# Hybrid SSD and attention layer on one core: 64-row tiles padded to 128 rows, the y half of the out-projection ahead of the norm, one-bank PSUM tiles, and a new issue order up to the FFN

## Chip, core and metric

The kernel runs on one core of one Trainium2 chip. The metric is the device time of one execution in microseconds (us). The engines are named as in the profile: PE (TensorE, matrix products), PEld (its weight loads), DVE (VectorE), ACT (ScalarE), POOL (GpSimd) and SP (SyncE, which here only issues DMAs).

## The reference

One layer is computed for 512 frames of a new stream and 64 frames of a running one, 576 tokens in all, with a model width of 1024:

```python
h = rmsnorm(x, p['norm_mix']);  proj = h @ p['w_in']          # z, xbc, dt, cq, ckv
xbc, conv_new = causal_conv(xbc, conv_buf, ...)               # 4 taps, then silu
y, h_new = ssd_scan(xh, dt, A, Bm, Cm, ssm_h0)                # 8 heads of 64, state 128
y = (y + d_skip * xh) * silu(z);  y_ssd = rmsnorm(y, p['ssd_norm'])
q = rmsnorm(cq, q_norm) @ p['w_uq'];  q_rope, k_rope = apply_rope(...)
o = mla_attend(...) @ w_uv                                    # 8 heads, keys: 256 cached + new
x = x + concat([y_ssd, o]) @ p['w_out']
x = x + (silu(hf @ w_gate) * (hf @ w_up)) @ w_down            # hf = rmsnorm(x), width 2816
```

The outputs are the normed x, the compressed keys, the rotated keys, the SSD states and the last rows ahead of the convolution. Everything is fp32.

## The kernel before

The activations lie transposed: channels on the 128 partitions, the 576 tokens along the free dimension. A product of full precision is made of three f32r matmuls: the weight and the activation are each split in a high and a low part, and high x high, high x low and low x high are added in PSUM (`product`, L123, and `product_halves`, L450). `split_weights` (L107) casts the high part on ACT and subtracts it on DVE for the low part. The SSD and the attention use plain fp32 matmuls.

The work runs in stages, each a string of step names that `steps` (L273) goes through:

- **Start and inputs (0 to about 87 us).** The first products with the norm of x (`norm_factor`, L189, gives R1), the small product for dt and the rotary key, then eight input tiles (`in_tile`, L285) with the convolution (`conv_tile`, L388), the step sizes (`step_sizes`, L342), and the rotary part of the queries (`q_rope`, L425). PSUM tiles come from a pool psA with two buffers of two banks each (`mm_tile`, L157): one tile holds both token halves, side by side.
- **SSD (to about 148 us).** Four z tiles and five chunks of 128 tokens, of which chunk 4, the running stream, has 64 (`chunk_a` L482, `chunk_e`, `chunk_b`, `chunk_s`); between them the first query and key projections of the attention (`pair_proj`).
- **Attention (to about 221 us).** `norm_y` (L758) makes the norm factor Ry of y, `cat_tile` (L763) multiplies y by gain and factor and splits it into cat_y. For each pair p of heads come the scores `S`, whose softmax (`soft`, L648) takes the maximum on DVE and the exponential on ACT; the transposes of the probabilities (`turn` T, `turn_s` t); the values (`values` V, `values_s` W). `F` is the y half of the out-projection for one of eight output tiles (`out_tile((0,), t)`, L738). PSUM has three banks for scores ("sc"), three for transposes and values ("pp") and two for projections ("hm"), each released by the DVE or ACT instruction that reads it. values_s works on 64 query rows; its first key block has 64 rows, the others 128.
- **Out-projection (to about 250 us)** with the attention half, added on x2 (loaded from x by SP, `load_x2` L769), and the y half of tile 1; beside it the FFN's first weight splits.
- **FFN (to about 597 us)** and the last product and norm. Nothing in these is changed.

The order in which each engine issues its instructions is written out: the table `ISSUE` holds, for each engine, the places of its instructions in program order, and `issue_in_order` (L1305) chains them. So an engine's queue is fixed, and an instruction that waits holds up what stands behind it on that engine.

## Time and profile before

| | |
|---|---|
| time, median of 3 runs | 635.02 us (634.54 to 635.94) |
| span of the profiled execution | 633.0 us |
| its PE busy time, share of the span | 622.7 us, 98% |
| DVE | 539.3 us, 85% |
| ACT | 400.4 us, 63% |
| POOL | 117.7 us, 19% |

What lies between the span and the median of the runs is 2.0 us. A row of the timeline has the start, the duration, the engine, the line, the operation, the tile written and the tiles read, the tile of the array (rows*columns), the shape and the count; a bracket at the end is the engine's idle time before it and what ended it. An fp32 matmul has two records in the trace.

### The profile page before, as it was taken

The numbers are of one execution on the slowest core, as the hardware profiler recorded it, in microseconds if no ns is written. First come the engines' busy times: TensorE is split into PE (matmuls) and PEld (weight loads), VectorE is DVE, ScalarE is ACT, GpSimd is POOL, SyncE is SP. The second block draws the span as 40 slices with busy tenths as digits, with TensorE's granted clock in tenths as the row PEclk, the third lists the DMA queues.
The fourth block names the chain that finished last, engine by engine and source line by source line (L and its number), as shares of the span: only waits on it lengthen the run. The fifth ranks groups of instructions, "written<-read, shape, count | busy, mean of one in ns | idle before, by whom it ended". The sixth has DMA issues, their size and how long they took to land.

```text
span 633.0 us, 12094 instructions
## 1 busy us (share of the span) xinstructions
PE 622.7 (98%) x4635; PEld 596.3 (94%) x4635; DVE 539.3 (85%) x939; ACT 400.4 (63%) x768; POOL 117.7 (19%) x170
## 2 busy tenths in 40 slices
PE   9999999999999999999999999999999999999995
PEld 9899999986787899999999999999999999999995
DVE  6999986789776699999999888988899789976555
ACT  7655346779775567666556676566657665767364
POOL 1322104231010000001301330033104220323323
PEclk9999999999999999999999999999999999999999
DMA  8322374413231223335743986397738893689924
GB/s 320 134 61 74 95 193 127 128 61 106 77 117 34 96 72 126 89 106 178 262 128 90 221 182 152 82 193 185 169 100 162 199 202 101 100 215 251 256 41 149
DMA packets 39593, 89.19 MB, mean 141 GB/s; under 512 B 4570, under 2 KB 14312, under 8 KB 39280
## 3 DMA queue, kind: packets, MB, share of 16 engines
q1 hardware_dynamic: 26416, 63.12, 31.0%
q0 software_dynamic: 12400, 24.73, 21.3%
q8 instruction: 36, 0.59, 0.4%
q10 hardware_dynamic: 720, 0.57, 0.3%
q14 instruction: 21, 0.17, 0.1%
HBM read 62.74 MB, written 24.53 MB: 138 GB/s over the span
## 4 chain that ended last, share of the span: by engine, by line
PE 88%; DVE 6%; ACT 2%; issue 2%; POOL 1%; DMA 1%; POOLq 0%; DVEq 0%
PE ps_x L874 21%; PE ps_d L1064 14%; PE ps_z L874 10%; PE ps_in L281 7%; PE ps_y L874 5%; PE ps_o L458 4%; PE ps_z L458 4%; PE ps_first L129 3%; PE ps_d L281 2%; PE sc L672 2%; PE ps_p L874 2%; PE ps_l L281 2%; PE pv L719 1%; PE ptp L694 1%; PE ps_q L458 1%
## 5 line engine op out<-in xcount | busy, mean ns | idle before, releaser
L874 PE MATMUL ps_x<-xop,wh_gu_S 128*128 128x288 f32 x378 | 76.9, 295 | 0.0
L112 DVE TENSOR_TENSOR wl_gu_S<-gu,wh_gu_S 128x1024 fp32r<-128x1024 f32 x44 | 53.3, 1220 | 9.1 <-ACT wh_gu_S L111 6.2
L874 PEld LDWEIGHTS ps_x<-xop,wh_gu_S 128*128 128x128 f32 x378 | 60.5, 188 | 0.0
L1078 POOL DMA_DIRECT2D acc<-fz x32 | 27.9, 902 | 166.5 <-ACT fz L1075 137.8
L111 ACT CAST wh_gu_S<-gu 128x1024 fp32r<-128x1024 f32 x44 | 46.3, 1053 | 16.3 <-PE ps_y L874 8.3
L874 PE MATMUL ps_x<-xop,wl_gu_S 128*128 128x288 f32 x189 | 55.8, 295 | 0.0
L281 PE MATMUL ps_in<-xs,wh_in 128*128 128x256 f32 (+1 forms) x256 | 51.2, 296 | 0.4 <-DVE sp_a L361 0.4
L281 PEld LDWEIGHTS ps_in<-xs,wh_in 128*128 128x128 f32 x256 | 40.8, 188 | 1.2 <-issue 1.1
L281 PE MATMUL ps_in<-xs,wl_in 128*128 128x320 f32 (+1 forms) x128 | 37.7, 295 | 0.0
L874 PEld LDWEIGHTS ps_x<-xop,wl_gu_S 128*128 128x128 f32 x189 | 35.6, 188 | 0.0
L111 ACT CAST wh_gu_A<-gu 128x1024 fp32r<-128x1024 f32 x22 | 23.1, 1050 | 10.6 <-PE ps_x L874 7.2
L874 PE MATMUL ps_z<-xop,gu_a 128*128 128x288 f32 x189 | 29.5, 294 | 0.0
L458 PE MATMUL ps_o<-cat_y,wh_out 128*128 128x256 f32 (+1 forms) x128 | 28.9, 311 | 0.5 <-DVE cat_y L145 0.3
L112 DVE TENSOR_TENSOR wl_gu_A<-gu,wh_gu_A 128x1024 fp32r<-128x1024 f32 x22 | 26.8, 1218 | 1.5 <-ACT wh_gu_A L111 1.3
L1023 POOL DMA_DIRECT2D acc<-dn x8 | 4.4, 544 | 121.5 <-ACT dn L1022 121.5
L874 PE MATMUL ps_x<-xop_last,wh_gu_S 128*128 128x288 f32 x126 | 26.9, 295 | 0.0
L874 PEld LDWEIGHTS ps_z<-xop,gu_a 128*128 128x128 f32 x189 | 26.5, 188 | 0.0
L1064 PE MATMUL ps_d<-pair,d_1h 128*128 128x288 f32 x128 | 26.4, 296 | 0.0
L874 PE MATMUL ps_z<-xop,wh_gu_S 128*128 128x288 f32 x126 | 26.0, 295 | 0.0
L458 PE MATMUL ps_z<-xs,wh_z 128*128 128x256 f32 (+1 forms) x128 | 25.8, 296 | 0.1
L874 PE MATMUL ps_y<-xop,wh_gu_A 128*128 128x288 f32 x126 | 25.8, 296 | 0.0
L458 PE MATMUL ps_o<-cat_o,wh_out 128*128 128x320 f32 (+1 forms) x128 | 25.4, 294 | 0.3 <-DVE x L750 0.3
(418 smaller groups left out, 2164.1 us busy)
## 6 DMA issues: line engine op xcount, KB each, us to landing
gu<-in_w_gu SPq DMA_DIRECT2D x44, 512.0 KB, 5.3
wr_d<-in_w_down SPq DMA_DIRECT2D x18, 512.0 KB, 4.2
acc<-fz POOLq DMA_DIRECT2D x16, 288.0 KB, 7.2
acc<-da POOLq DMA_DIRECT2D x16, 288.0 KB, 8.0
acc<-dc POOLq DMA_DIRECT2D x16, 288.0 KB, 8.5
wr_in<-in_w_in SPq DMA_DIRECT2D x8, 512.0 KB, 3.8
wr_out<-in_w_out SPq DMA_DIRECT2D x8, 512.0 KB, 3.4
cumb<-cumD SPq DMA_DIRECT2D x5, 512.0 KB, 4.0
```

The costliest lines, as they stand in the source:

```text
L111: act.copy(hi, raw)
L112: dve.tensor_tensor(lo, raw, hi.bitcast(F32), ALU.subtract)
L129: pe.matmul(ps[:m, hf, : cols.stop - cols.start], w, x[:, cols], start=start and k == 0 and i == 0, stop=stop and k == last and i == 2,)
L281: pe.matmul(ps, w, x[:, cols], start=first and k == 0 and i == 0, stop=last and k == len(terms) - 1 and i == 2,)
L458: pe.matmul(ps[:, :n], w, x[:, cols], start=k == 0 and i == 0, stop=k == len(terms) - 1 and i == 2,)
L672: pe.matmul(s[:, :nk], qs[:, j, q0 : q0 + P], ks[:, j, :nk], start=True, stop=True)
L694: pe.transpose(pp[:, k : k + P], prs[p, i][:, j, b * P : b * P + P], ident)
L719: pe.matmul(pv[64 * j : 64 * j + 64, b * P :], V[b][:, h * HD : (h + 1) * HD], pts[p, b, j], start=b == 0, stop=True, skip_group_check=b > 0,)
L874: pe.matmul(ps, p, q, start=not onto and first and kp == kps[0] and j == 0, stop=onto or (last and kp == kps[-1] and j == 2), skip_group_c ...
L1023: pool.dma_start(acc[1][t], dn)
L1064: pe.matmul(ps, p, v, start=not onto and n == 0 and j == 0, stop=onto or (n == len(ks) - 1 and j == 2), skip_group_check=onto,)
L1078: pool.dma_start(out, src, accum_op=ALU.add)
```

## The change

1. **Padding.** Tiles with 64 rows get 128. The probabilities of the running stream's first key block get 64 rows of zeros (once, by POOL) and its V tile 128 rows, so values_s multiplies 128 rows; chunk 4 of the SSD takes the last 128 tokens (`window`), with the step sizes of the first 64 of them set to 0; the transposes to dt become products with a zero-padded k1.
2. **y half.** cat_tile splits y times the gain without the factor Ry; the evacuation of F multiplies by Ry, and x is added afterwards by a DMA with accumulation from POOL's queue, one per output tile, in place of two loads by SP. F1 is made in the attention too.
3. **PSUM.** psA holds four tiles of one bank; the input tiles, q_rope's products and the first norm use pairs of them, and q_rope and that norm work half by half.
4. **Order.** The places in ISSUE are new on all engines up to the FFN.

```diff
-    psA_, psA = open_pool("psA", bufs=2, space=PSUM)
+    psA_, psA = open_pool("psA", bufs=4, space=PSUM)
...
     def mm_tile(name):
-        return psA.tile([P, 2, 512], F32, tag="mm", name=name)
+        return psA.tile([P, 512], F32, tag="mm", name=name)
+
+    def mm_pair(name):
+        return [mm_tile(f"{name}_{hf}") for hf in range(2)]
...
+    def window(c):
+
+        t0 = min(c * P, T - P)
+        return slice(t0, t0 + P)
...
-            pe.transpose(pdt[:n, c * 24 : c * 24 + 24], k1[0:24, c * P : c * P + n], ident[:24, :24])
+            pe.matmul(pdt[:, c * 24 : c * 24 + 24], k1[:, window(c)], ident[:, :24], start=True, stop=True)
...
-        for i, (f, g, u, op) in enumerate(((c0, c1, qt0, ALU.subtract), (c1, c0, qt1, ALU.add))):
-            dve.tensor_tensor(halves(s[:, i]), rr[0], f, ALU.mult)
-            dve.tensor_tensor(halves(u), rr[1], g, ALU.mult)
-            dve.tensor_tensor(s[:, i], s[:, i], u, op)
+        for hf, cols in enumerate(HC):
+            for i, (f, g, u, op) in enumerate(((0, 1, qt0, ALU.subtract), (1, 0, qt1, ALU.add))):
+                dve.tensor_tensor(s[:, i, cols], rr[0][hf][:, :TH], cs[:, f, cols], ALU.mult)
+                dve.tensor_tensor(u[:, cols], rr[1][hf][:, :TH], cs[:, g, cols], ALU.mult)
+                dve.tensor_tensor(s[:, i, cols], s[:, i, cols], u[:, cols], op)
...
-                    pv[64 * j : 64 * j + 64], V[4 + b][:kn, h * HD : (h + 1) * HD],
-                    pts[p, 4][:kn, b * P + j * TS : b * P + j * TS + TS], start=b == 0, stop=b == 2,
+                    pv[64 * j : 64 * j + 64], V[4 + b][:, h * HD : (h + 1) * HD],
+                    pt_s[:, b * P + j * TS : b * P + j * TS + TS], start=b == 0, stop=b == 2,
...
         def evac(ps, cols):
-            dve.tensor_tensor(x2[t][:, cols], ps, x2[t][:, cols], ALU.add)
+            y = x2[t][:, cols]
+            if hfs[0]:
+                dve.tensor_tensor(y, ps, y, ALU.add)
+            else:
+                dve.tensor_tensor(y, ps, Ry[:, cols], ALU.mult)
 
         product_halves(terms, UNEVEN, f"ps_o{hfs[-1]}_{t}", evac)
+        if not hfs[0]:
+            pool.dma_start(x2[t], a["xT"][:, t], accum_op=ALU.add)
...
     def cat_tile(t):
-        dve.scalar_tensor_tensor(xsd[:, t], xsd[:, t], col(C_SN + t), Ry, ALU.mult, ALU.mult)
         s = slot(ypool, "a1", f"cat_y{t}")
-        split_scaled(s, xsd[:, t], None)
+        split_scaled(s, xsd[:, t], col(C_SN + t))
...
-            sp.dma_start(z, a["xT"][:, 4 * i2 : 4 * i2 + 4])
...
     def last_out(t):
-        hfs = (1,) if t in begun else (0, 1)
+        hfs = (1,)
```

One line of PE's table of places: `-154-169 174-175 170-171 270-274 176-221 172-173 222-269 275-370 373-420 371 421-468 372 469-634 637 641-644 638-640` becomes `+154-169 174-175 170-171 176-221 172-173 222-312 323-324 313 325-326 347-351 327 314-316 352-358 317 359 328-329 318` and so on. What it does is seen better in the queues.

**PE, the scores of pairs 0 and 1.** At about 150 us PE had the last scores of pair 0 (sc_0), the running stream's (sc_s), the scores of pair 1 (sc_3, sc_2), then the transposes (ptp), and the first product of the y half (ps_o) behind them:

```order
L672 MATMUL sc_0_0_1994<-ks_382,qs_381 128x128
L672 MATMUL sc_0_1_1996<-ks_382,qs_381 128x128
L678 MATMUL sc_s<-ks_382,qs_381 64x320 x2
L672 MATMUL sc_3_0_2018<-ks_384,qs_383 128x512
L672 MATMUL sc_3_1_2020<-ks_384,qs_383 128x512
L672 MATMUL sc_2_0_2060<-ks_384,qs_383 128x384
L694 MATMUL ptp_0_0_2037<-ident,pr_0_2000 128x128
L694 MATMUL ptp_0_0_2037<-ident,pr_1_1972 128x128
L694 MATMUL ptp_0_0_2037<-ident,pr_2_1986 128x128
L694 MATMUL ptp_0_0_2037<-ident,pr_3_1946 128x128
L458 MATMUL ps_o_0_0_2116<-cat_y_1955,wh_out_0_2112 128x256
L694 MATMUL ptp_0_1_2043<-ident,pr_0_2000 128x128
```

and now (ps_g are the sums for the norm factor):

```order
L597 MATMUL ps_g_1904<-ysq_1902,ones 128x128
L685 MATMUL sc_0_1_2022<-ks_393,qs_392 128x128
L691 MATMUL sc_s<-ks_393,qs_392 64x320 x2
L685 MATMUL sc_3_0_2044<-ks_395,qs_394 128x512
L468 MATMUL ps_o_0_0_2138<-cat_y_1983,wh_out_0_2134 128x256
L707 MATMUL ptp_0_0_2062<-ident,pr_0_2026 128x128
L707 MATMUL ptp_0_0_2062<-ident,pr_1_1998 128x128
L707 MATMUL ptp_0_1_2068<-ident,pr_0_2026 128x128
L685 MATMUL sc_3_1_2046<-ks_395,qs_394 128x512
L468 MATMUL ps_o_0_1_2152<-cat_y_1983,wh_out_0_2134 128x320
L685 MATMUL sc_2_0_2082<-ks_395,qs_394 128x384
```

Products of the y half (ps_o_0_0, ps_o_0_1) stand between the scores of pair 1 and among the transposes of pair 0, and sums for the norm factor stand behind scores.

**DVE, the same place.** The maximum of pair 1's first scores (mx<-sc_3_0) stood behind the norm factor Ry and the first product with it (L764), among the splits of y (cat_y):

```order
L178 TENSOR_TENSOR nr_u<-nr_u,nr_v 128x288
L657 RECIPROCAL sm<-sm 128x2
L179 SCALAR_TENSOR_TENSOR Ry<-nr_u,nr_y 128x288
L662 TENSOR_SCALAR pr_0_2000<-pr_0_2000,sm 128x128
L764 SCALAR_TENSOR_TENSOR xsd<-xsd,par,Ry 128x576
L657 RECIPROCAL sm<-sm 128x1
L655 TENSOR_REDUCE mx<-sc_3_0_2018 128x1
L764 SCALAR_TENSOR_TENSOR xsd<-xsd,par,Ry 128x576
L662 TENSOR_SCALAR pr_4_2013<-pr_4_2013,sm 128x320
L764 SCALAR_TENSOR_TENSOR xsd<-xsd,par,Ry 128x576
L145 TENSOR_TENSOR cat_y_1955<-xsd,cat_y_1955 128x576
L764 SCALAR_TENSOR_TENSOR xsd<-xsd,par,Ry 128x576
```

and now:

```order
L668 TENSOR_REDUCE mx<-sc_3_0_2044 128x1
L670 RECIPROCAL sm<-sm 128x1
L177 TENSOR_SCALAR nr_v<-R_98 128x288
L668 TENSOR_REDUCE mx<-sc_3_1_2046 128x1
L675 TENSOR_SCALAR pr_4_2039<-pr_4_2039,sm 128x320
L668 TENSOR_REDUCE mx<-sc_2_0_2082 128x1
L147 SCALAR_TENSOR_TENSOR cat_y_1986<-xsd,par,cat_y_1986 128x576
L182 TENSOR_TENSOR nr_u<-nr_u,nr_v 128x288
L147 SCALAR_TENSOR_TENSOR cat_y_1989<-xsd,par,cat_y_1989 128x576
L183 SCALAR_TENSOR_TENSOR Ry<-nr_u,nr_y 128x288
L147 SCALAR_TENSOR_TENSOR cat_y_2058<-xsd,par,cat_y_2058 128x576
L112 TENSOR_TENSOR wl_pair_2269<-wr_pair_2266,wh_pair_2268 128x384
```

The products with Ry are gone, the three maxima of pair 1 stand ahead of the later splits (L147), and Ry is made between these.

**PE, the values of pair 1.** pv are the values of the new stream, pvs those of the running one; x2 are the two heads of a pair, each with half of the array's columns. Before:

```order
L719 MATMUL pv_2439<-pt_0_2342,V_1660 64x512 x2
L719 MATMUL pv_2439<-pt_1_2253,V_1660 64x384 x2
L719 MATMUL pv_2439<-pt_2_2331,V_1671 64x256 x2
L719 MATMUL pv_2439<-pt_2_2331,V_1671 64x128 x2
L730 MATMUL pvs_2451<-pts_2432,V_1682 64x64 x4
L730 MATMUL pvs_2451<-pts_2432,V_1693 64x64 x2
```

and now:

```order
L730 MATMUL pv_2463<-pt_0_2366,V_1687 64x512
L741 MATMUL pvs_2475<-pts,V_1709 64x64 x2
L730 MATMUL pv_2463<-pt_0_2366,V_1687 64x512
L730 MATMUL pv_2463<-pt_1_2276,V_1687 64x384 x2
L730 MATMUL pv_2463<-pt_2_2355,V_1698 64x256 x2
L741 MATMUL pvs_2475<-pts,V_1709 64x64 x2
L741 MATMUL pvs_2475<-pts,V_1720 64x64 x2
L730 MATMUL pv_2463<-pt_2_2355,V_1698 64x128 x2
```

Two pvs stand between the two heads' products of 512 columns, and the others ahead of the last pair of pv.

**DVE, out-projection and start of the FFN.** ps_o_1_0 and ps_o_1_1 are the two token parts of output tile 1; wl are weight splits, xv and xop the FFN's operands. Before, tile 1 had one evacuation per part (L750):

```order
L750 TENSOR_TENSOR x_0_2049<-ps_o_0_0_2795,x_0_2049 128x256
L833 TENSOR_TENSOR gu_2_2878<-gu_2_2878,gu_0_2876 128x512
L832 TENSOR_TENSOR gu_3_2879<-gu_1_2877,gu_0_2876 128x512
L834 TENSOR_TENSOR gu_3_2879<-gu_0_2876,gu_2_2878 128x512
L112 TENSOR_TENSOR wl_gu_A_2889<-gu_0_2876,wh_gu_A_2888 128x1024
L750 TENSOR_TENSOR x_0_2049<-ps_o_0_1_2809,x_0_2049 128x320
L842 TENSOR_TENSOR gu_a_2886<-gu_1_2877,gu_a_2886 128x512
L112 TENSOR_TENSOR wl_gu_S_2893<-gu_2_2878,wh_gu_S_2892 128x1024
L750 TENSOR_TENSOR x_0_2049<-ps_o_1_0_2823,x_0_2049 128x256
L822 TENSOR_TENSOR xop<-xv_0_2936,xop 128x288
L112 TENSOR_TENSOR wl_gu_S_2897<-gu_3_2879,wh_gu_S_2896 128x1024
```

and now it has one from the attention's end (L764, with Ry) and one more here (L762), which comes after the DMA that adds x:

```order
L764 TENSOR_TENSOR x_0_2074<-ps_o_1_0_2781,Ry 128x256
L847 TENSOR_TENSOR gu_2_2909<-gu_2_2909,gu_0_2907 128x512
L764 TENSOR_TENSOR x_0_2074<-ps_o_1_1_2795,Ry 128x320
L112 TENSOR_TENSOR wl_gu_A_2920<-gu_0_2907,wh_gu_A_2919 128x1024
L762 TENSOR_TENSOR x_0_2074<-ps_o_0_0_2850,x_0_2074 128x256
L848 TENSOR_TENSOR gu_3_2910<-gu_0_2907,gu_2_2909 128x512
L112 TENSOR_TENSOR wl_gu_S_2924<-gu_2_2909,wh_gu_S_2923 128x1024
L762 TENSOR_TENSOR x_0_2074<-ps_o_0_1_2864,x_0_2074 128x320
L112 TENSOR_TENSOR wl_gu_S_2928<-gu_3_2910,wh_gu_S_2927 128x1024
L762 TENSOR_TENSOR x_0_2074<-ps_o_1_0_2878,x_0_2074 128x256
L856 TENSOR_TENSOR gu_a_2917<-gu_1_2908,gu_a_2917 128x512
L762 TENSOR_TENSOR x_0_2074<-ps_o_1_1_2892,x_0_2074 128x320
```

Between the two evacuations of the first part stand the second part's, weight splits and the evacuations of tile 0.

More of the change, by code (lines that the diff above doesn't have):

```diff
@@ L189, in norm_factor @@
     def norm_factor(R, ps, n):
-        norm_half(halves(R), ps[:, :, :TH], n, halves)
+        if not isinstance(ps, list):
+            norm_half(halves(R), ps[:, :, :TH], n, halves)
+            return
+        for hf in range(2):
+            norm_half(R[:, hf * TH : (hf + 1) * TH], ps[hf][:, :TH], n, part=f"{hf}_")
     HC = [slice(hf * TH, (hf + 1) * TH) for hf in range(2)]
@@ L200, in hybrid_layer_kernel @@
     R1h = halves(R1)
[L201 removed]
+    pss = [psS.tile([P, 2, 512], F32, name=f"ps_first{i}") for i in range(2)] + [mm_pair("ps_first2")]
     warm = mm_tile("ps_warm")
     for i in range(8):
[L205 removed]
+        pe.matmul(warm[:, :P], ones, ones, start=True, stop=True)
     xsd, bc, sz = (midp.tile([P, 4, T], F32, tag=z, name=z) for z in ("xsd", "bc", "sz"))
@@ L646, in hybrid_layer_kernel @@
     prs, pts = {}, {}
+    pt_s = ap_.tile([P, 3 * P], F32, name="pts")
+    pool.memset(pt_s[TS:, :P], 0.0)
     def soft(p, i, scs, nk):
```

293 lines of the change are left out of this document (154 added, 139 removed).

## The prediction

> **What bounds the kernel now.** I read the page's busy times and its chain first, then the stretches one by one, then PE's own waits, and last the timeline of the one stretch in which PE stops.
>
> ```profile
> PE 622.7 (98%) x4635; PEld 596.3 (94%) x4635; DVE 539.3 (85%) x939; ACT 400.4 (63%) x768; POOL 117.7 (19%) x170
> PE 88%; DVE 6%; ACT 2%; issue 2%; POOL 1%; DMA 1%; POOLq 0%; DVEq 0%
> ```
>
> PE is busy for 622.7 of 633.0 us and carries 88% of the chain that ended last. So the change can win only in two ways: it fills the places where PE stands still, or it makes PE's own stream shorter. DVE, at 539.3 us, is the engine that can spoil it. The columns of the windows below are PE, PE's weight loads, DVE, ACT and POOL, each with its instructions in brackets.
>
> ```profile
> 26.00:86.00 60.00, 59.60 (x449) 56.67 (x446) 55.79 (x111) 28.46 (x45) 16.35 (x37) 1.00 0.29 84
> 150.00:162.00 12.00, 10.31 (x56) 6.61 (x54) 11.94 (x29) 10.38 (x30) 1.99 (x4) 1.00 0.51 170
> 162.00:182.00 20.00, 20.00 (x135) 15.50 (x134) 14.32 (x35) 14.30 (x39) 1.95 (x4) 1.00 0.28 94
> 222.00:250.00 28.00, 27.57 (x208) 27.14 (x207) 27.69 (x51) 20.00 (x32) 0.00 (x0) 1.00 0.29 95
> 260.00:280.00 20.00, 19.99 (x148) 19.55 (x147) 19.81 (x35) 13.60 (x24) 0.00 (x0) 1.00 0.33 97
> ```
>
> Only one stretch is loose: 150 to 162 us, the norm of y, the split of y and the scores of pairs 0 and 1. PE has 10.31 of 12 us there while DVE has 11.94. From 162 on PE is full and DVE has room; from 222 on both are full, since the FFN's weight splits begin. The clock is 1.00 everywhere, so it plays no part. PE's waits up to 250 us name the same place.
>
> ```profile
> PE sc L672 <- ACT pr L656: 1.1, 2, 0.9
> PE ps_in L281 <- DVE sp_a L361: 0.4, 1, 0.4
> PE ps_o L458 <- DVE cat_y L145: 0.3, 1, 0.3
> PE ps_o L458 <- DVE x L750: 0.3, 1, 0.3
> ```
>
> **What the loose stretch is worth.** A matmul that waits inside its pipeline shows as busy, so I count starts.
>
> ```profile
> 150.88 0.90 PE L672 MATMUL sc<-ks,qs 100*128 100x128 f32 x4
> 152.01 0.76 PE L678 MATMUL sc_s<-ks,qs 100*64 100x320 f32 x4 [0.23 <-ACT pr L656]
> 153.67 1.98 PE L672 MATMUL sc<-ks,qs 100*128 100x512 f32 x4 [0.90 <-ACT pr L656]
> 155.86 0.91 PE L672 MATMUL sc<-ks,qs 100*128 100x384 f32 x2 [0.21 <-ACT pr L656]
> 156.61 0.60 PE L694 MATMUL ptp<-ident,pr 128*128 128x128 f32 x4
> 157.23 0.39 PE L458 MATMUL ps_o<-cat_y,wh_out 128*128 128x256 f32 x1
> ```
>
> Between 150.88 and 157.23 us, 6.35 us, PE starts 4 x 128 + 4 x 320 + 4 x 512 + 2 x 384 + 4 x 128 = 5120 columns. The price of 128 fp32 columns is 0.11 us, from this block of attention values (its second row):
>
> ```profile
> 215.38 0.33 PE L730 MATMUL pvs<-pts,V 64*64 64x64 f32 x4
> 215.64 2.38 PE L719 MATMUL pv<-pt,V 128*64 128x512 f32 x16
> 217.85 0.40 PE L730 MATMUL pvs<-pts,V 128*64 128x64 f32 x8
> 218.18 0.39 PE L458 MATMUL ps_o<-cat_y,wh_out 128*128 128x256 f32 x1
> ```
>
> Its 16 matmuls are 4 each of 512, 384, 256 and 128 columns, 5120 in all, and take 217.85 - 215.64 = 2.21 us. That is 0.055 us per 128 columns, because they are half arrays (128*64) that run two by two; one alone costs 0.11. So 5120 full-array columns are 40 x 0.11 = 4.4 us, and 6.35 - 4.4 = 1.95 us are lost. With the 0.3 us on cat_y and the 0.3 us on x (both wait for work that the y norm pushed late), 2.55 us stand to be won at most. DVE's rows there say why the change can win them (138 to 162 us):
>
> ```profile
> L764 DVE SCALAR_TENSOR_TENSOR xsd<-xsd,par,Ry 128x576 f32<-128x576 f32 x4 | 3.2, 809 | 0.0
> L145 DVE TENSOR_TENSOR cat_y<-xsd,cat_y 128x576 fp32r<-128x576 f32 x4 | 2.8, 750 | 0.0
> ```
>
> The four multiplications by the norm factor, 3.2 us, vanish: the factor now rides on the evacuation of the products, which DVE makes anyway. Before, the maximum of the next scores stood in DVE's queue behind factor, multiplication and split; now it stands ahead of three of the splits, and the first products of the y half no longer wait for the norm, so PE has them between the scores. 3.2 us taken from a queue that holds PE up for 2.55 us is enough; ACT, at 10.38 of 12 us, is the next to be late. I take **-2.5 us**, since PE has other work at each of these places, with bounds -2.55 and 0 (if ACT's exponentials set the pace).
>
> **Padding to 128 rows.** In the block above the first 4 matmuls (64*64) take 215.64 - 215.38 = 0.26 us for two pairs of 64 columns, whose share at the price above is 2 x 0.055 = 0.11; the 8 that follow (128*64) take 0.33 for four pairs, 0.22. What is over, 0.11 to 0.15 us, is the change of tile size, in and out. The other kind of block has it twice in one run:
>
> ```profile
> 197.84 0.71 PE L730 MATMUL pvs<-pts,V 64*64 64x64 f32 x12
> 198.48 0.41 PE L458 MATMUL ps_o<-cat_y,wh_out 128*128 128x320 f32 x1
> ```
>
> 12 matmuls, six pairs, take 0.64 us where 0.33 would do. With the 64-row form gone, each of four blocks saves 0.2 to 0.3, and chunk 4 of the SSD and the transposes to dt save as many changes again in small: **-1.2 us**, bounds -1.5 and -0.5. The added rows cost PE nothing, since a matmul's time here goes by its columns. The Trainium skill, "TensorEngine Tiling (Array Packing)", Key Properties, says that changing the tiling mode drains the TensorE; the 0.1 us or so per change agrees. The same section says that different tiles execute in parallel, which speaks against padding, as 64-row tiles could share the array; by it the sum would lose a few tenths, but the 64*64 rows above show no such gain (0.26 us for two pairs is not below 0.11).
>
> **The split pairs.** The new order puts pvs matmuls between the two halves of a pv pair (512 columns once in pairs 1 and 2, 384 once in pairs 0 and 2, 256 and 128 in pair 3). In before, only pair 0 had one, of 256:
>
> ```profile
> 167.86 2.15 PE L719 MATMUL pv<-pt,V 128*64 128x512 f32 x10
> 171.13 0.70 PE L678 MATMUL sc_s<-ks,qs 100*64 100x320 f32 x3
> ```
>
> It took 171.13 - 167.86 = 3.27 us against 218.18 - 215.38 = 2.80 for pair 3, 0.47 more. Each fp32 matmul stands twice in the trace (16 rows for 8), so a half of 256 columns that runs alone takes 4 x 0.11 = 0.44: the split cost what its first half took alone, with the 64*64 rows between the halves. If every new split cost as much, it would be 2 x (512 + 512 + 384 + 384 + 256 + 128 - 256) = 3840 columns, 30 x 0.11 = 3.3 us; if the halves still overlap, 0, since now no change of tile size stands between them and pvs of the other half can fill the free columns. I take **+0.9**, nearer to the lower end for that reason.
>
> **Transposes and scores among f32r products.** The new order has about 70 more such interleavings before 250 us (counted in the two orders). One of them:
>
> ```profile
> 162.60 0.31 PE L458 MATMUL ps_o<-cat_y,wh_out 128*128 128x320 f32 x1
> 162.75 0.49 PE L694 MATMUL ptp<-ident,pr 128*128 128x128 f32 x3
> 162.99 0.40 PE L458 MATMUL ps_o<-cat_y,wh_out 128*128 128x320 f32 x1
> 163.23 0.31 PE L458 MATMUL ps_o<-cat_y,wl_out 128*128 128x320 f32 x1
> ```
>
> 163.23 - 162.60 = 0.63 us for two f32r of 320 (0.15 each, by the first start to the next) and three transposes (0.33): nothing to 0.01 us over. So **+0.6 us**, bounds 0 and +0.7.
>
> **The y half's last product.** F1 moves from the out-projection, where its 12 terms shared one bank with the other half, to the end of attention. PE's work is the same, but it now has an evacuation of its own:
>
> ```profile
> 162.51 0.42 DVE L750 TENSOR_TENSOR x<-ps_o,x 128x256 f32<-128x256 f32 x1
> 163.57 0.49 DVE L750 TENSOR_TENSOR x<-ps_o,x 128x320 f32<-128x320 f32 x1
> ```
>
> That is 0.91 us more on DVE in a stretch where it has 28.00 - 27.69 = 0.31 us free and PE waits for its weight splits next: **+0.4 us**, bounds 0 and +0.6.
>
> **x by accumulating DMA.** Two loads leave SP; eight accumulating DMAs join POOL's queue, each behind its tile's evacuation. POOL is at 0.00 us from 222 to 250, so issuing is hidden. The out-projection's evacuation of tile 1 must wait for the last of them. The nearest rows are accumulating DMAs of the same size, in quiet and in a loaded stretch, and POOL's four small issues:
>
> ```profile
> acc<-x POOLq DMA_DIRECT2D x8, 288.0 KB, 3.7
> acc<-dc POOLq DMA_DIRECT2D x16, 288.0 KB, 8.5
> 153.06 2.02 POOL L616 DMA_DIRECT2D qs<-rrp  x4 [11.49 <-PE sc_s L678]
> ```
>
> Between the evacuation that releases the DMA and the one that needs it, the new order has three weight splits and two evacuations on DVE, by their rows 3 x 1.22 + 0.42 + 0.49 = 4.6 us, and one addition more. The DMA needs 0.5 us of issue and 3.7: **0**, upper bound 0.5 + 8.5 - 4.6 = +4.4. The split's row:
>
> ```profile
> L112 DVE TENSOR_TENSOR wl_gu_S<-gu,wh_gu_S 128x1024 fp32r<-128x1024 f32 x44 | 53.3, 1220 | 9.1 <-ACT wh_gu_S L111 6.2
> ```
>
> The page "DMA: Bandwidth & Descriptors" of the Trainium skill, section "Anatomy of one DMA", fits 2.0 us plus bytes / 436e3; by that the landing would be an estimated 2.7 us, and the sum stays the same.
>
> **One-bank tiles, rope, norm.** Banks of the inputs come free singly, and their order weaves up to three input tiles. PE's wait there is 0.4 us; DVE, at 55.79 of 60, gets six more half operations in the rope (0.5 us) and the norm halves (0.4). I take **-0.3**, bounds -0.6 and +1.0. The late copies of the conv state on POOL cost nothing as long as its 16.35 of 60 us leave room.
>
> **Sum.** -2.5 - 1.2 + 0.9 + 0.6 + 0.4 + 0 - 0.3 = -2.1 us on the span, 633.0 to 630.9. The median of the runs, 635.02, is 2.0 above the span, so the time is 632.9.
>
> **Rivals.** (A) *The accumulating DMA is late*: with a landing of 6 to 8.5 us DVE stops at the head of its queue for 1.9 to 4.4 us, the weight splits behind it are late, and PE with its two banks stops too. For it: DMA bursts in this stretch; against it: 3.7 us in the nearest row. It gives 632.9 + 1.9 = 634.8 to 632.9 + 4.4 = 637.3, and it decides above a landing of 4.1 us. (B) *Slower: the norm factor comes late.* Its last sums now stand behind the scores in PE's order, its logarithm behind exponentials on ACT; DVE, which is in order, waits for it ahead of an evacuation of transposes and of later maxima. If each of the two factor halves holds DVE for 2 us in a stretch where ACT has 1.6 of 12 us free, 4 us come back in place of the 2.5 that were won: 632.9 + 4.0 = 636.9. It decides once the waits come to over 636.29 - 632.9 = 3.4 us. (C) *More gain*: pairs lose nothing, nothing new waits: 0.9 + 0.6 + 0.4 = 1.9 more than forecast, and with the input banks at their bound of -0.6 another 0.3: 630.7. (D) *The change does not fill the stretch*, because ACT's exponentials free the score banks no sooner: the 2.5 stay, 635.4. The chances: forecast 0.45, A 0.14, B 0.16, C 0.15, D 0.10.
>
> **How the numbers follow.** A measurement of this kernel tells 0.2%, 1.27 us, from no change. The forecast, 632.9, lies 2.1 below 635.02, so 0.38 of its 0.45 is faster and 0.07 the same; C is faster; A is 0.09 the same and 0.05 slower; D is the same; B is slower. Faster 0.53, same 0.26, slower 0.21. The forecast's own range is 631.3 to 635.3, the lower end with the split pairs and the interleavings at 0, the upper with the split pairs at 3.3. The range of 8 in 10 takes in C down to a little below its value and A nearly to its end: 630.3 to 636.8, which leaves out most of B and a little of A and C.
>
> **What would show it.** Right: in the changed profile the scores' waits for ACT in the loose stretch shrink below 0.5 us, PE has over 11.5 of 12 us there, no 64*64 row is left, and the pv blocks are longer. Wrong: a PE or DVE wait for x's DMA at the out-projection (A), DVE idle ahead of the norm factor (B), or a stretch that still has 2 us of holes (D). If the time before 222 us shrinks but PE's wait at the start of the FFN grows, the gain was given back to DVE.

## The result, and the profile after

The changed kernel takes **643.4 us** (median of 4 runs, 643.17 to 643.98) against 634.82 us for the kernel before, measured beside it (4 runs, 634.54 to 635.94): a ratio of 1.0133, 95% interval 1.0121 to 1.0146. It is 8.6 us slower; the prediction had said 632.9 us, 630.3 to 636.8. The profiled execution has a span of 641.5 us, 8.4 more than before.

The page's first part and its row of TensorE's granted clock, in 40 slices, for the changed kernel:

```profile
PE 627.0 (98%) x4640; PEld 601.3 (94%) x4640; DVE 538.3 (84%) x945; ACT 401.2 (63%) x771; POOL 126.5 (20%) x180
...
PEclk9989999999999999999999999999999999999998
...
PE 79%; DVE 7%; issue 5%; ACT 3%; POOL 2%; DMA 2%; POOLq 0%; SPq 0%; DVEq 0%; ACTq 0%
```

PE is busy 4.3 us longer, and its share of the chain that ended last fell from 88% to 79%. In the third slice, 32 to 48 us, the clock is not full. The windows that the prediction had read, in the changed kernel (PE, PE's weight loads, DVE, ACT, POOL, then clock):

```profile
26.00:86.00 60.00, 56.85 (x415) 53.95 (x414) 52.36 (x105) 27.15 (x43) 14.34 (x30) 0.97 0.22 66
...
150.00:162.00 12.00, 11.54 (x59) 8.32 (x58) 10.86 (x29) 11.42 (x33) 1.10 (x2) 1.00 0.13 40
...
222.00:250.00 28.00, 26.68 (x206) 24.89 (x205) 22.84 (x42) 15.58 (x23) 2.58 (x3) 1.00 0.57 145
```

The stretch that the change was to fill is fuller, 11.54 of 12 us against 10.31. But PE lost 2.75 us among the inputs (56.85 against 59.60 of 60) and 0.9 at the entry of the FFN. PE's waits up to 262 us:

```profile
PE ps_in L290 <- DVE cq L272: 3.1, 1, 3.1
PE ps_o L468 <- DVE x L764: 1.2, 1, 1.2
...
PE ps_z L468 <- DVE qt L446: 0.7, 1, 0.7
PE ps_x L507 <- DVE qt L446: 0.4, 1, 0.4
...
PE sc_s L691 <- ACT pr L669: 0.3, 1, 0.3
```

The scores' wait of 1.1 us for ACT is gone, and new ones stand in its place. (Not shown are a wait of 1.1 us at the very start, which was there before, and a new one of 0.3 us, in which the sums for the norm factor wait for ACT.) The largest, 3.1 us, names DVE's cq, but cq was only late. DVE's timeline there:

```profile
29.51 1.43 DVE L112 TENSOR_TENSOR wl_in<-wr_in,wh_in 128x1024 fp32r<-128x1024 f32 x1 [1.69 <-ACT wh_in L111]
35.18 1.37 DVE L320 TENSOR_TENSOR k<-ps_small,R 24x288 f32<-24x288 f32 x3 [4.24 <-POOL k L305]
36.59 0.82 DVE L272 TENSOR_TENSOR cq<-ps_first,R 128x288 f32<-128x288 f32 x2
```

DVE stood still for 4.24 us, for POOL's k of line 305. That is the memset of k1, which the padded transposes to dt need. POOL's timeline of the same stretch:

```profile
26.34 0.72 POOL L432 DMA_DIRECT2D krall<-in_cache_kropeT  x1 [22.72 <-DVE R L183]
27.18 1.15 POOL L251 TENSOR_SCALAR_AFFINE_SELECT qs<-qs 4x1152 f32<-4x1152 f32 x1
...
29.82 2.14 POOL L251 TENSOR_SCALAR_AFFINE_SELECT qs<-qs 4x1152 f32<-4x1152 f32 x1
...
34.00 0.52 POOL L255 DMA_DIRECT2D ks<-ks  x1
34.56 0.59 POOL L305 MEMSET k<- 128x576 f32 x1
```

The memset takes 0.59 us, and it stands behind a DMA that waited for the first norm factor, four selects and two more DMAs. DVE writes the rows of k1 after it, in order; cq stands behind that, and PE's bank behind cq. When PE started again it ran at half speed for 3.4 us:

```profile
37.10 0.89 PE L290 MATMUL ps_in<-xs,wh_in 128*128 128x320 f32 x2 [3.15 <-DVE cq L272]
...
38.06 0.74 PE L290 MATMUL ps_in<-xs,wh_in 128*128 128x320 f32 x2
38.59 0.47 PE L290 MATMUL ps_in<-xs,wl_in 128*128 128x320 f32 x1
...
40.95 0.46 PE L290 MATMUL ps_in<-xs,wh_in 128*128 128x320 f32 x2
41.24 0.31 PE L290 MATMUL ps_in<-xs,wl_in 128*128 128x320 f32 x1
```

Two products of 320 columns take 38.59 - 38.06 = 0.53 us there and 41.24 - 40.95 = 0.29 us afterwards.

Where the time went, by the starts of matmuls in the profiled executions (us between the first ps_in, the first ps_z, the first scores, the first attention values, the last ones, and the FFN's first product ps_p; the last six columns are experiments, told below):

| stretch | before | after | e1 | e7 | e9 | e12 | e8 | e14 |
|---|---|---|---|---|---|---|---|---|
| inputs (ps_in to ps_z) | 57.56 | 63.30 | 59.78 | 58.98 | 59.12 | 58.86 | 57.47 | 57.48 |
| z and chunks (to the scores) | 57.09 | 58.43 | 58.18 | 57.57 | 57.75 | 57.60 | 60.49 | 57.21 |
| scores (to the values) | 23.52 | 22.29 | 22.27 | 22.30 | 22.30 | 22.26 | 24.05 | 23.55 |
| first to last values | 50.17 | 50.64 | 50.60 | 50.63 | 50.66 | 52.16 | 49.18 | 49.22 |
| out-projection (to ps_p) | 23.51 | 25.19 | 24.88 | 25.47 | 24.79 | 24.77 | 23.52 | 23.51 |
| from ps_p to the last matmul | 385.87 | 385.96 | 386.68 | 385.92 | 385.73 | 385.59 | 386.49 | 385.88 |

Of the 8.4 us, 5.7 are lost in the inputs and 1.7 at the out-projection. The scores win 1.2, and the stretches around them lose 1.3 and 0.5. Each column is one execution: the last row, in which nothing was changed, differs by up to 1.1 us between them, so a few tenths in one column prove little by themselves. The scores' 24.05 us in e8 are a matter of the clock, to which the last section comes.

### The profile page after: what moved, and what is told of

It is laid out like the page before. It is cut to its first block, busy times and chain, and to the rows that moved or that the text cites. A ratio compares the mean times of both kernels' runs of the same rounds, so it can differ in the third digit from the quotient of the medians.

```text
span 641.5 us, 12138 instructions
## 1 busy us (share of the span) xinstructions
PE 627.0 (98%) x4640; PEld 601.3 (94%) x4640; DVE 538.3 (84%) x945; ACT 401.2 (63%) x771; POOL 126.5 (20%) x180
## 4 chain that ended last, share of the span: by engine, by line
PE 79%; DVE 7%; issue 5%; ACT 3%; POOL 2%; DMA 2%; POOLq 0%; SPq 0%; DVEq 0%; ACTq 0%
PE ps_x L888 21%; PE ps_d L1078 14%; PE ps_z L888 10%; PE ps_in L290 8%; PE ps_y L888 5%; PE ps_z L468 3%; PE ps_o L468 3%; PE ps_first L129 2%; PE sc L685 2%; PE ps_d L290 2%; PE ps_l L290 2%; PE ptp L707 1%; DVE xop L836 1%; PE ps_q L468 1%; PE ps_k L468 1%
## 5 line engine op out<-in xcount | busy, mean ns | idle before, releaser
L290 PE MATMUL ps_in<-xs,wl_in 128*128 128x256 f32 (+1 forms) x128 | 35.7, 301 | 0.0
L468 PE MATMUL ps_o<-cat_y,wh_out 128*128 128x256 f32 (+1 forms) x128 | 32.6, 336 | 0.0
L468 PE MATMUL ps_z<-xs,wh_z 128*128 128x256 f32 (+1 forms) x128 | 27.9, 307 | 0.7 <-DVE qt L446 0.7
L468 PE MATMUL ps_o<-cat_o,wh_out 128*128 128x256 f32 (+1 forms) x128 | 25.5, 297 | 1.3 <-DVE x L764 1.2
L888 PE MATMUL ps_x<-xop,wh_gu_A 128*128 128x288 f32 x126 | 25.7, 295 | 0.0
```

Source lines behind the costliest of these rows:

```text
L290: pe.matmul(ps, w, x[:, cols], start=first and k == 0 and i == 0, stop=last and k == len(terms) - 1 and i == 2,)
L468: pe.matmul(ps[:, :n], w, x[:, cols], start=k == 0 and i == 0, stop=k == len(terms) - 1 and i == 2,)
L888: pe.matmul(ps, p, q, start=not onto and first and kp == kps[0] and j == 0, stop=onto or (last and kp == kps[-1] and j == 2), skip_group_c ...
```

## The experiments

Each median below stands against the kernel before, measured beside it: 635.08 us beside e1, e2, e3 and e5, 635.06 beside e6 to e9, 635.02 beside e10, e12 and e13, 635.11 beside e14. These differ by less than 0.1 us, so the medians can be set side by side. Where an edit is a row of the issue order, the lines are the kernel's program rows, - for the old place and + for the new.

**The memset alone.** e1_memset_first is the changed kernel with one row of POOL moved:

```
 L432 DMA krall<-in_cache_kropeT 32x256
+L305 MEMSET k_425 128x576
 L251 AFFINE_SELECT qs_392<-qs_392 4x1152
...
 L255 DMA ks_395<-ks_393 4x1664
-L305 MEMSET k_425 128x576
```

> The changed kernel with one instruction moved: POOL zeroes k1 directly behind its first DMA, ahead of the four selects, instead of behind them and two DMAs. Theory (DVE stood still for 4.2 us behind that zeroing, PE for 3.2 us behind DVE, and the clock was lower for 3.4 us after it): the multiplication of k starts near 30 us instead of 35.2, PE's wait on cq goes, no stretch has a clock under 0.99, and the time falls by 4.7 to 6 us, to 637.4 to 638.7. Rival (the input stage is bound by DVE's work under the new order, the zeroing only shows it): the wait moves to another DVE instruction and the time falls by less than 1.5 us.

Measured: 639.44 us (638.96 to 639.57), ratio 1.0067 [1.0054, 1.0079]. Moving one row of 0.58 us gave 4.0 us back. POOL and DVE in the profile of e1, two views:

```profile
26.92 0.58 POOL L305 MEMSET k<- 128x576 f32 x1
```

```profile
29.35 2.00 DVE L112 TENSOR_TENSOR wl_in<-wr_in,wh_in 128x1024 fp32r<-128x1024 f32 x1 [1.68 <-ACT wh_in L111]
31.27 1.37 DVE L320 TENSOR_TENSOR k<-ps_small,R 24x288 f32<-24x288 f32 x3
```

DVE reaches k at 31.27 us and no longer waits for POOL, and PE's 3.1 us of waiting are gone. The gain is 0.7 us short of the range that was expected; two smaller waits that PE meets now, from the list of its waits in e1, add up to as much:

```profile
PE ps_in L290 <- DVE sp_q L370: 0.5, 1, 0.5
...
PE ps_in L290 <- DVE up L406: 0.2, 1, 0.2
```

e5_before_late_memset puts the same memset, for which nothing has a use, into the kernel before, at the late place in POOL's order:

```
 )
+pool.memset(k1, 0.0)
```

> The kernel before with one instruction added: POOL zeroes k1 behind its selects and the two DMAs after them, where the changed kernel has it; nothing else needs it here. Theory: DVE waits for it until about 34 us, PE stands still for 2 to 4 us near 31 us, the clock drops for some us, and the time rises by 3 to 6 us over before. Rival (harmless by itself): within 0.6 us of before.

Measured: 641.29 us (640.33 to 642.29), ratio 1.0098 [1.0085, 1.0112], 6.2 us slower, a little above what was expected. PE's waits and one window of that profile:

```profile
PE ps_dt L347 <- DVE k L311: 4.0, 2, 3.3
```

```profile
26.00:42.00 16.00, 12.03 (x71) 9.36 (x68) 10.94 (x22) 4.59 (x8) 7.66 (x8) 0.79 0.15 43
```

4.0 us of waiting, and a mean clock of 0.79 over 16 us. The two runs show it from both sides: one late row on POOL, an engine that is 80% idle, costs 4 to 6 us. The other half, 639.44 - 635.08 = 4.4 us, is something else.

**The split pairs.** e2_pairs_kept is e1 with each pv pair kept together in PE's order; one of the places:

```
-L730 MATMUL pv_2463<-pt_0_2366,V_1687 64x512
-L741 MATMUL pvs_2475<-pts,V_1709 64x64 x2
-L730 MATMUL pv_2463<-pt_0_2366,V_1687 64x512
+L730 MATMUL pv_2463<-pt_0_2366,V_1687 64x512 x2
```

> As e1, and on PE the pv and pvs matmuls of each pair of heads stand in the order of before, so that the two halves of each pv pair follow each other. Theory (split pairs run one after the other, in part): the blocks of values shorten by 0.2 to 0.8 us each in pairs 1 and 2, the time is 0.5 to 1.2 us under e1. Rival (halves overlap across what stands between them): within 0.3 us of e1.

Measured: 639.12 us (638.93 to 639.54), 0.3 below e1, and the stretch from the first to the last values is as long as in e1 (50.67 against 50.60 us). The split costs nothing that these runs can tell.

**The entry of the FFN.** e3_f1_evac_ahead is e1 with the two evacuations of F1 ahead of the weight sums in DVE's order:

```
+L764 TENSOR_TENSOR x_0_2074<-ps_o_1_0_2781,Ry 128x256
 L845 TENSOR_TENSOR gu_2_2909<-gu_1_2908 128x512
 L112 TENSOR_TENSOR wl_out_2_2935<-wr_out_2_2932,wh_out_2_2934 128x1024
+L764 TENSOR_TENSOR x_0_2074<-ps_o_1_1_2795,Ry 128x320
 L846 TENSOR_TENSOR gu_3_2910<-gu_1_2908,gu_0_2907 128x512
-L764 TENSOR_TENSOR x_0_2074<-ps_o_1_0_2781,Ry 128x256
 L847 TENSOR_TENSOR gu_2_2909<-gu_2_2909,gu_0_2907 128x512
-L764 TENSOR_TENSOR x_0_2074<-ps_o_1_1_2795,Ry 128x320
```

> As e1, and on DVE the two evacuations of the y half's last product (F1) stand ahead of the first operations on the FFN's weights, one of which waits for a DMA. Theory (that DMA wait stands ahead of F1's evacuation and holds PE's bank): PE's wait of 1.2 us on x at the start of the out-projection goes, and the time is 0.7 to 1.3 us under e1. Rival (DVE's work from here to the FFN sets the time, whatever its order): the wait comes back at the FFN's first products and the time is within 0.4 us of e1.

Measured: 638.65 us (638.53 to 639.25), 0.8 below e1; but the trace doesn't put that gain where the edit is. From the last values to ps_p it takes 24.99 us against 24.88, while the unchanged part from ps_p on is 1.1 us shorter (385.55 against 386.68) and the inputs 0.5 (59.32 against 59.78). PE's wait there only moved on, from the evacuations of F1 (L764, 1.2 us) to those of the next tile:

```profile
PE ps_o L468 <- DVE x L762: 1.1, 2, 0.6
```

**dt, rope query and entry, one after another.** e6_dt_transposes is e1 without the padding of the transposes to dt, and so without the memset:

```
-    pool.memset(k1, 0.0)
-            pe.matmul(pdt[:, c * 24 : c * 24 + 24], k1[:, window(c)], ident[:, :24], start=True, stop=True)
+            pe.transpose(pdt[:, c * 24 : c * 24 + 24], k1[0:24, window(c)], ident[:24, :24])
```

> The early-memset kernel (639.4 us) with the step sizes turned by five 24-row transposes again, over the shifted windows, so that k1 needs no memset at all. Theory: the ten records of the plain product, 1.03 us against 0.41 us in the kernel before, were paid on TensorE's path: 638.6 to 639.0 us. Rival: the time there is set by VectorE's and ScalarE's step-size chain, and TensorE's 0.6 us is given back at the next wait: 639.3 to 639.6 us, with a longer wait in the input stage.

Measured: 639.67 us (638.37 to 640.09), ratio 1.0062 [1.0049, 1.0075]: no gain. The rival was right, and a longer wait in the inputs shows it (two of e6's waits at the inputs; in e1 the first was 0.5 us and the second wasn't there):

```profile
PE ps_in L290 <- DVE sp_q L369: 0.7, 1, 0.7
PE ps_in L290 <- ACT wh_uqr L111: 0.5, 1, 0.5
```

e7_qrope_evac_early is e6 with three of the rope query's evacuations earlier on DVE:

```
+L445 TENSOR_TENSOR qt_430<-ps_qr_0_1154,cos_sin 128x288
+L445 TENSOR_TENSOR qt_431<-ps_qr_0_1154,cos_sin 128x288
 L405 TENSOR_TENSOR up_1129<-ps_in_0_1079,R_98 128x256
...
+L445 TENSOR_TENSOR qt_431<-ps_qr_1_1155,cos_sin 128x288
 L407 TENSOR_TENSOR up_1129<-ps_in_1_1080,R_98 128x64
```

> The kernel of the run before in this list, with three of VectorE's rope-query products (those that empty the second product's two banks) issued earlier: two ahead of the last input tile's evacuation, one ahead of the split of a z weight and the last convolution. Theory: the waits of 0.7 us ahead of ps_z and 0.4 us ahead of ps_x are these late evacuations and go: 637.5 to 638.1 us. Rival: the evacuation of the last input tile, now later, or the split of the z weight holds TensorE in their place: no more than 0.3 us gained, and a wait of 0.5 us or more on another operation of VectorE at 87 to 96 us.

Measured: 638.55 us (637.95 to 641.02), ratio 1.0058 [1.0044, 1.0071]: 1.1 us below e6, but half a microsecond short of the theory's range. The wait ahead of ps_x is gone (the stretch to the scores went from 58.52 us in e6 to 57.57); the one ahead of ps_z is still 0.6. DVE's row at that place, in the profile of e9 below, which has the same order there, says why:

```profile
88.13 0.82 DVE L445 TENSOR_TENSOR qt<-ps_qr,cos_sin 128x288 f32<-128x288 f32 x2 [1.05 <-PE ps_qr L129]
```

DVE is there early and waits 1.05 us for PE's own rope product, whose bank the first z tile takes over: the product comes too late in PE's order, and nothing stands between it and z. No run moved it.

e9_out_entry is e7 with e3's edit and the evacuations of the next tile earlier as well:

```
+L761 TENSOR_TENSOR x_0_2073<-ps_o_0_0_2849,x_0_2073 128x256
 L112 TENSOR_TENSOR wl_gu_A_2919<-gu_0_2906,wh_gu_A_2918 128x1024
-L761 TENSOR_TENSOR x_0_2073<-ps_o_0_0_2849,x_0_2073 128x256
 L847 TENSOR_TENSOR gu_3_2909<-gu_0_2906,gu_2_2908 128x512
+L761 TENSOR_TENSOR x_0_2073<-ps_o_0_1_2863,x_0_2073 128x320
 L112 TENSOR_TENSOR wl_gu_S_2923<-gu_2_2908,wh_gu_S_2922 128x1024
-L761 TENSOR_TENSOR x_0_2073<-ps_o_0_1_2863,x_0_2073 128x320
```

> The kernel of the run before in this list, with VectorE's evacuations of y-half tile 1 and of the first whole out-projection tile ahead of the feed-forward weights' sums and splits. Theory: at the entry of the feed-forward part the cost is VectorE's order (1.2 us of waits of TensorE), so 1.0 to 1.5 us go: 636.2 to 637.0 us, and the first feed-forward product starts 1 us earlier relative to the last attention product. Rival: the evacuation moved earlier waits for the accumulating DMA of tile 1 or 0, or the splits moved back hold the first feed-forward products: at most 0.4 us gained, and VectorE shows a wait on that DMA of over 1 us.

Measured: 637.8 us (637.76 to 638.4), ratio 1.0044 [1.0032, 1.0056], 0.75 below e7, between the theory's range and the rival's. The out-projection takes 24.79 us against 25.47 in e7 and 23.51 before. No wait of DVE for the accumulating DMAs is left there; PE's waits in e9 at the out-projection, and at the inputs:

```profile
PE ps_o L467 <- DVE x L761: 0.9, 2, 0.7
PE ps_in L290 <- DVE sp_q L369: 0.7, 1, 0.7
PE ps_z L467 <- DVE qt L445: 0.6, 1, 0.6
...
PE ps_in L290 <- DVE up L405: 0.3, 1, 0.3
```

DVE's queue is the likely cause of what is left at the out-projection: from 224.5 to 234 us it works without a pause on weight sums, splits and evacuations, two of which F1 has added. No run took F1 back to its old place, so this is argued and not shown.

**The interleavings.** In the kernel before PE goes back from plain fp32 operations to products of split weights 14 times between the first and the last values, in the changed one 44 times, and 45 times instead of 11 from the first z tile to the scores. e12_turns_grouped gathers the turns (ptp) of e9, one place of many:

```
+L467 MATMUL ps_o_2_1_2339<-cat_y_1985,wl_out_2_2322 128x320
+L467 MATMUL ps_o_2_1_2339<-cat_y_1988,wh_out_2_2321 128x320
 L706 MATMUL ptp_1_0_2276<-ident,pr_1_2101 128x128
 L706 MATMUL ptp_1_0_2276<-ident,pr_2_2087 128x128
-L467 MATMUL ps_o_2_1_2339<-cat_y_1985,wl_out_2_2322 128x320
 L706 MATMUL ptp_1_1_2281<-ident,pr_1_2101 128x128
-L467 MATMUL ps_o_2_1_2339<-cat_y_1988,wh_out_2_2321 128x320
```

> The kernel with the three repairs (637.8 us) with one change: from the first attention values on, TensorE's turns of the probabilities (ptp) are gathered, each held back behind at most six products of the out-projection, up to the next other plain fp32 operation. Returns from plain fp32 operations to products of split weights between the first and the last attention values: 14 in the kernel before, 44 in the changed kernel, 25 here. Theory: each such return costs 0.06 to 0.08 us (in the traces the second product behind it starts 0.09 us late), so that 19 fewer give 1.1 to 1.5 us: 636.3 to 636.8 us, all in the stretch from the first to the last attention values. Rival: interleaving is free, as its single steps overlap, and a turn held back makes the values or VectorE late: 637.6 us or more.

Measured: 639.6 us (638.05 to 639.86), ratio 1.0072 [1.0058, 1.0085]: 1.8 us slower than e9 in place of 1.1 to 1.5 faster. The stretch of the values is 1.5 us longer (52.16 against 50.66), and the two waits that are new in it, 0.5 and 0.3 us, don't cover that. e13_all_grouped is e12 with the chunks' operations gathered in the same way:

```
-L506 MATMUL ps_x_1276<-ident,xsd 128x128
 L467 MATMUL ps_z_1_1241<-xs_273,wh_z_1209 128x320
 L467 MATMUL ps_z_0_1215<-xs_335,wh_z_1209 128x256
+L467 MATMUL ps_z_1_1241<-xs_273,wl_z_1210 128x320
+L506 MATMUL ps_x_1276<-ident,xsd 128x128
```

> The run before in this list, with the plain fp32 operations of the chunks (turns, scan products and gate sums, from the first z tile to the first scores) gathered in the same way, each held back behind at most three products of split weights: 26 returns in that part, 45 in the changed kernel, 12 in the kernel before. Theory: 19 returns fewer at 0.06 to 0.08 us: another 1.1 to 1.5 us, to 634.9 to 635.7 us, where the kernel before stands. Rival: the chain of the chunks from TensorE through VectorE and ScalarE and back is what that part waits for, and each operation held back by up to 0.45 us makes the next one late: no gain or a loss, 636.5 to 637.5 us, with waits of TensorE on VectorE or ScalarE at 92 to 145 us.

Measured: 646.62 us (645.73 to 647.87), ratio 1.0184 [1.017, 1.0198]: 7 us slower again. Nothing of the gain is seen that a price of 0.06 to 0.08 us per return would give. The rival has the reason, but not the size: its 636.5 to 637.5 us are missed by 9. The first line below is the longer of e12's two new waits among the values; the second fence has e13's waits for ACT, the longest of its list:

```profile
PE ps_q L467 <- ACT ks L636: 0.5, 1, 0.5
```

```profile
PE ps_v L615 <- ACT V L616: 3.6, 4, 1.9
PE ps_q L467 <- ACT ks L636: 1.1, 2, 0.6
```

Operations held back by less than half a microsecond each make PE wait for ACT for 4.7 us: single plain operations among the products are what the chains through ACT and DVE need. So the interleaving isn't shown as the price that was sought; what it costs without such waits, these two runs don't tell.

**The padding alone.** e8_before_padding is the kernel before, in its own order, with the padding of chunk 4, of the last key block and of its values, but not of dt; from its diff:

```
-            pe.transpose(px[:L, t * P : t * P + P], xsd[:, t, tk], ident)
+            pe.transpose(px[:, t * P : t * P + P], xsd[:, t, tw], ident)
...
-                    pv[64 * j : 64 * j + 64], V[4 + b][:kn, h * HD : (h + 1) * HD],
-                    pts[p, 4][:kn, b * P + j * TS : b * P + j * TS + TS], start=b == 0, stop=b == 2,
+                    pv[64 * j : 64 * j + 64], V[4 + b][:, h * HD : (h + 1) * HD],
+                    pt_s[:, b * P + j * TS : b * P + j * TS + TS], start=b == 0, stop=b == 2,
```

> The kernel before, in its own order, with only the padding of the last chunk, of the last key block and of its values (the step sizes keep their 24-row transposes, so no memset of k1; one small memset for the padded weights' rows). What the prediction took for the padding, less its part in the step sizes: 0.6 to 1.0 us faster, 634.0 to 634.5 us. Theory now: the padded rows and columns have to be streamed and cost what the spared mode changes give back: within 0.4 us of the kernel before. A third case: the columns added by the shifted windows cost as priced by the columns, 0.6 us slower.

Measured: 636.34 us (12 runs, 635.62 to 638.79), ratio 1.0022 [1.0012, 1.0032]: slower by more than any of the three cases. The values' stretch is 1.0 us shorter, as the first case wants, and PE waits at another place, here PE's timeline and the windows of that place:

```profile
93.56 0.33 PE L510 MATMUL ps_b<-bc 128*128 128x64 f32 x2
96.15 0.44 PE L509 MATMUL ps_b<-ident,bc 128*128 128x128 f32 x1 [2.25 <-DVE bc L413]
```

```profile
96.00:98.00 2.00, 1.85 (x10) 1.85 (x11) 1.83 (x3) 0.00 (x0) 2.00 (x6) 0.55 0.34 65
98.00:100.00 2.00, 2.00 (x12) 2.00 (x12) 1.03 (x2) 0.34 (x2) 1.62 (x3) 0.59 0.64 90
```

The shifted window of chunk 4 covers the last 64 tokens of the prompt too, and these come out of the convolution's long part (L413), which the order of before gives to DVE last. The new order had taken care of it. (The profiled execution, 638.42 us, is one of two at 638.4 and 638.8; the other ten took 635.6 to 636.7, so the clock seems not to fall in each of them.) e10_before_padding_conv moves these two operations, e14_before_padding_zh also the evacuation that was late next:

```
 L414 SCALAR_TENSOR_TENSOR bc<-cth_1052,cacc_1047 128x64
+L413 SCALAR_TENSOR_TENSOR bc<-cth_1052,cacc_1047 128x512
 L407 SCALAR_TENSOR_TENSOR cacc_1119<-up_1111,hcw,cacc_1119 128x579
 L414 SCALAR_TENSOR_TENSOR bc<-cth_1124,cacc_1119 128x64
+L413 SCALAR_TENSOR_TENSOR bc<-cth_1124,cacc_1119 128x512
```

> The kernel before with the padding alone, as in the padding run that showed TensorE waiting 2.25 us for the convolution's long part of the last two tiles, whose last 64 columns the shifted window now needs; VectorE now issues these two operations 1.9 us earlier, each right behind the short part of its tile. Theory: that wait, and the 0.9 us at a clock of 0.70 to 0.80 behind it, hid a gain of the padding of about 0.5 to 1.1 us (the attention values' stretch was 1.0 us shorter there): 633.9 to 634.6 us. Rival: the padding gains nothing, since its added columns cost what the spared changes of shape give: 634.9 to 635.4 us.

Measured: 634.92 us (11 runs, 634.34 to 636.03), ratio 0.9998 [0.9989, 1.0007]: as fast as before. The wait for L413 is gone, and the next one has come:

```profile
PE ps_z L462 <- DVE zh L472: 0.9, 1, 0.9
```

```
+L472 SCALAR_TENSOR_TENSOR zh_1187<-ps_z_0_1189,R_98 128x256
 L441 TENSOR_TENSOR rrp<-rrp,qt_418 128x576
 L441 TENSOR_TENSOR rrp<-rrp,qt_419 128x576
-L472 SCALAR_TENSOR_TENSOR zh_1187<-ps_z_0_1189,R_98 128x256
```

> The padding alone on the kernel before, as in the run of 634.92 us, with one more operation of VectorE moved: the evacuation of the first z bank is issued ahead of the two rope-query sums (L441, 1.42 us) that stood in front of it when TensorE waited 0.86 us for it. Theory: the padding is worth about 0.9 us (1.0 us in the attention values' stretch) less its added columns in the last chunk, and what hid that in the run of 634.92 us is this wait: 634.0 to 634.5 us, that is 0.6 to 0.9 us faster than the kernel before, the fastest kernel of this study. Rival: the padding is worth nothing, and the wait only goes elsewhere: 634.8 to 635.2 us, with a wait of TensorE of 0.5 us or more on another operation between 93 and 105 us.

Measured: 633.97 us (11 runs, 633.46 to 635.18), ratio **0.9984** [0.9975, 0.9993]. This is the fastest kernel of the study: 1.1 us faster than the kernel before and 9.4 faster than the changed one. The values of pair 2 in PE's timeline of e14, which answer to the 0.71 us row of before:

```profile
197.56 0.52 PE L735 MATMUL pvs<-pts,V 128*64 128x64 f32 x12
198.01 0.42 PE L462 MATMUL ps_o<-cat_y,wh_out 128*128 128x320 f32 x1
```

198.01 - 197.56 = 0.45 us for the 12 matmuls that took 0.64.

## Why the prediction was wrong, point by point

**The step that failed** first is the one on POOL: the sum has no term for the memset of k1. The padding part says that the added rows "cost PE nothing", and that is so; but it lists what the padding spares and not the instruction that it adds. The one sentence on POOL in the part on the inputs, that its work "cost nothing as long as its 16.35 of 60 us leave room", takes an engine's share for its queue's order. POOL had room in the 60 us, and not in the 9 us (26.3 to 35.2) in which its answer was wanted. It cost 4.0 us (e1 against after), shown by e1 and e5. In the changed kernel's profile it is 3.1 us of waiting and 1.7 of half clock, 4.8; of these the inputs of e1 got 3.5 back (63.30 to 59.78 us), and its two new waits are another 0.7. On the clock the prediction wrote "The clock is 1.00 everywhere, so it plays no part", which was true of the windows that it had read and untrue of a kernel in which PE stops for 3 us. Without this step the change would still have missed: e1's 639.44 us lies above the range's 636.8, 4.4 over the kernel before where 2.1 under it was forecast. The rest is in three more terms, one-bank tiles, scores and F1, told next.

**One-bank tiles, rope, norm: -0.3, bounds -0.6 and +1.0.** Sign and size wrong, even without the memset. The inputs took 59.78 us in e1 and 59.12 in e9 against 57.56, and the late evacuation of a rope bank cost 0.4 more at ps_x. Cut in halves, each bank of the rope query has two readers on DVE, and the last of them sets when PE gets the bank back; e7 got 1.1 us back by their order alone. 1.6 us remain in e9; 1.2 of them are waits of 0.7, 0.6 and 0.3 us at places where before had one of 0.4. The late rope product explains the 0.6; why the other two came is not shown.

**The padding: -1.2.** Right in size, when the order fits: -1.1 (e14, interval -1.6 to -0.4), nearly all of it among the values (49.22 against 50.17 us), as the prediction's 0.2 to 0.3 for each of four blocks has it. What it added for chunk 4 doesn't show (57.21 against 57.09 us). Not foreseen was that the shifted window waits for other operations than the 64 rows did: 2.4 us of e8's time hang on the order of three rows of DVE. The dt part had the wrong sign: PE's five products to dt in the changed kernel are ten records of 0.11 us, 1.03 from the first start to the start of the next operation, and the five transposes before took 0.42. e6 shows that this time is hidden.

**The split pairs: +0.9.** Nothing can be measured (e2). The lower bound was right, as it would be if the halves overlap what lies between them.

**The scores' stretch: -2.5.** The mechanism was right, by the signs that the prediction had named: the scores' wait for ACT is 0.3 us (sc_s alone), PE has 11.54 of 12 us, no 64*64 row is left. The stretch got 1.2 us shorter, and it has more work than before: six products for a query (ps_q, 0.13 us each by their starts) that stood among the chunks stand in it now, 0.8 us. So for the same work it wins 2.0 of the 2.5. (The hole itself was larger than the 1.95 us that the prediction worked out. It took the running stream's scores, 4 x 320 columns in tiles of 100*64, as full arrays; by its own price of half arrays they are 0.55 us less, and 2.5 us were lost there.)

What failed is that the rest of the part stays as it was: the stretches next to the scores got longer. From the first z tile to the last values e9 takes 130.70 us and before 130.78, though e14, with the padding (without dt) and three moved rows of DVE, takes 129.98. So the y half and the order together lose 0.7 us there in place of winning 1.0 (-2.5 + 0.9 + 0.6). Against e14 the values lose 1.4 us (50.66 against 49.22), of which two more products of the out-projection are about 0.2, and the z tiles and chunks lose 0.5 (57.75 against 57.21) although they have 0.8 us less to do, so 1.3. Keeping the pairs together (e2) or gathering the turns (e12) brings none of it back, and which of the moved rows it is stays open in both stretches.

**Interleavings: +0.6.** Not shown on its own: the two runs that took interleavings away brought new waits and lost time. The 1.3 us of the z tiles and chunks, which have 45 returns in place of 11, leave room for it.

**F1 at the entry: +0.4, bound +0.6.** Mis-sized: the out-projection lost 1.7 us in the changed kernel, 1.3 in e9, if all of that is F1's. That DVE would be the one to spoil it was right: PE's wait at the start of the FFN grew, the prediction's sign for it, though the time before 222 us didn't shrink. The prediction counted DVE's 0.91 us of added evacuations against its free time, not the place in which they stand, behind sums that wait for a DMA; DVE's waits in the changed kernel from 222 to 262 us:

```profile
DVE x L764 <- PE ps_o L468: 3.6, 2, 3.3
DVE gu L845 <- DMA gu<-in_w_gu: 1.1, 1, 1.1
DVE x L762 <- DMA x<-in_xT: 0.5, 1, 0.5
```

**The accumulating DMA: 0, and rival A.** The third line is rival A, with 0.5 us. The landing was above its point of 4.1 us, as the DMA view of 215 to 262 us has it:

```profile
x<-in_xT POOLq DMA_DIRECT2D x4, 288.0 KB, 5.2
```

By its own sum that is 0.5 + 5.2 - 4.6 = 1.1 us of DVE, of which it cost DVE half, at a place where other waits stood already. The fit of the Trainium skill that the prediction quoted from "DMA: Bandwidth & Descriptors" gives 2.7 us; the measurement decides, and here it is twice that.

**Rivals B and D** didn't come: among the waits of DVE and PE from 140 to 222 us none is for the norm factor Ry, and the stretch was filled. **C** was right on the pairs and wrong in "nothing new waits". The forecast's own range should begin at 631.4 by its terms (632.9 - 0.9 - 0.6), not 631.3, which changes nothing. The rival that did come, another engine's queue ahead of DVE, wasn't on the list.
